# Order of 32 experts written out by hand: first products of one expert around the second products of the one before

## Chip, cores, metric

One core of a Trainium2 chip runs the whole program. Times are device microseconds (us) of one execution; lower is better. Engines: TensorE (PE; its weight loads are PEld), VectorE (DVE), ScalarE (ACT), GpSimd (POOL) and SyncE (SP), which issues the transfers of the weights.

## What is computed

The program is a block of mixed attention with a mixture of experts, and two further layers behind it. The change lies in the mixture: 256 tokens, 32 experts, each token goes to 4 of them. Cut to what matters (`expert_block` works on a block of an expert's tokens):

```python
def expert_block(args):
    tok_idx, e = args
    xb = t_pad[tok_idx]
    hb = xb @ w_exp_in[e] + b_exp_in[e]
    g = jnp.minimum(hb[:, :D_FF], SWIGLU_LIMIT)
    u = jnp.clip(hb[:, D_FF:], -SWIGLU_LIMIT, SWIGLU_LIMIT)
    a = g * jax.nn.sigmoid(SWIGLU_ALPHA * g) * (u + 1.0)
    return a @ w_exp_out[e] + b_exp_out[e]
...
y = jnp.einsum('nk,nkd->nd', gate_w, y_slot)
```

Everything is float32; D_MODEL and D_FF are 1024, so `w_exp_in[e]` has 8.4 MB and `w_exp_out[e]` 4.2 MB. All 32 experts are read once: 403 MB of the 593 MB that the program reads.

## The kernel before

**Work of one expert.** An expert takes up to 64 tokens (CAP). `gather` (L873) picks the tokens' columns out of h1 with matmuls by a selection that VectorE makes, for two experts at a time; the result `xg` is the stationary operand of the first products. `expert` (L905) then does, in the order of its code: `spread_sel` (L892: the selection `sd` back to the tokens with the gate weights, on VectorE, two transposes, a copy `sTs`); the bias into two PSUM banks `pg` and `pu` (L767, 8 matmul instructions); the first products (L915), 64 instructions over four weight tiles `tin`; the clamped SwiGLU (L932 to L938: gc, sg, sg, uc, uc, four on VectorE and one on ScalarE); four transposes of uc (L943, `aT`) and their copy `aTs` (ScalarE, L946); the second products (L951, `py`), 32 instructions over two weight tiles `tout`; their copy `ys` (L954); and the combination (L959, `pc`), 8 instructions whose four banks VectorE adds to `facc` (L964; facc lies in the tensor bcs). A float32 matmul is two instructions in the trace, and the two halves of 64 columns run beside each other.

**Buffers.** PSUM has four banks with tag "b" and four with tag "g" (`pg` and `pu` of two experts). A weight tile is [128, 4096] float32, 2 MB. Eight buffers hold them: `ring` (3), `ring2` (4) and `ring3` (1). `w_exp` (L834) hands out the tiles of an expert, the four tin and then the two tout, and `pick` (L838) takes the buffers by a pattern with period eight; from tile 119 on, ahead of the loop, another pattern. One tile of expert 1 (`spare`, L855) goes into other memory. SP issues the transfers in order (`wload`, L127, L135), and an issue waits until the products that read the buffer's last tile are done.

**What sets the order.** The engines' instructions are put in order by a scheduler at build time; `keep` pins an instruction behind the one traced before it on its engine, and `tc.issue_after(i)` puts a block's instructions behind `i` on its engine. The expert stage pins nearly nothing beside the first eight tiles. `pairs_of` (L1095) calls `expert` for e0 to e1 and puts the gathering for the next pair behind the first quarter of the first products of the pair's first expert. Beside the experts stand: `facc_init` and the gathering for expert 1 (behind the products of expert 0), `later_consts` (L1020, constants on VectorE for later stages, after pair 0), `load_bo` (expert 2), `ln2_rows` (expert 4, rows spread by matmuls, L994) and `out_bias` (expert 6, L1006).

**The loop.** An expert with more than 64 tokens needs further blocks. A loop `tc.For_i(0, n_over, 1)` (L1126) stands after expert 19; its number of iterations is read from the chip, and is 0 for these inputs. Its weight tiles go into `ring2`, all four buffers of it, so ahead of it only three tiles of expert 20 are asked for (L1123), all in `ring`:

```python
    xg = pairs_of(0, 20, xg)
    got = [f() for f in w_exp(20)[0:3]]
    ...
    with tc.For_i(0, n_over, 1) as it:
        ...
        tin, tout = w_all(w_exp(eo, only2=True))
        ...
    pairs_of(20, NE, xg, got)
```

Behind expert 31 the sums of its combination start from facc by matmuls (`take_sum`, L923), and three tiles of the next stage follow (L1146).

Of the kernel before, what the change touches and what calls it, by code (L numbers as in the profile page):

```python
# [9 lines left out]
F32 = mybir.dt.float32  # L10
# [8 lines left out]
NE = 32  # L19
# [53 lines left out]
def tile_kernel(  # L73
# [691 lines left out]
    def expert_bias(p, oh, q, pin=lambda i: i, halves=(0, 1)):  # L765
        for hv in halves:
            pin(T.matmul(p[64 * hv:64 * hv + 64, :], oh[:, q + hv:q + hv + 1].to_broadcast([128, 64]), bi,  # L767
                         start=True, stop=False))

    def first_bias(e, i, halves=(0, 1)):  # L770
        expert_bias(first_acc[e][i], ident[:, 4 * e:4 * e + 4], 2 * i, keep, halves)
# [62 lines left out]
    def w_exp(e, only2=False):  # L834
        wi = w_exp_in[0, e] if isinstance(e, int) else w_exp_in[0, ds(e, 1)].rearrange("o k n -> (o k) n")
        wo_ = w_exp_out[0, e] if isinstance(e, int) else w_exp_out[0, ds(e, 1)].rearrange("o k n -> (o k) n")

        def pick():  # L838
            if only2:
                return ring2  # L840
            m = n_tile[0]
            n_tile[0] += 1
            return (ring2, ring, ring2, ring2, ring, ring3, ring, ring2)[m % 8] if m < 119 else (
                ring, ring, ring, ring2, ring2, ring3, ring2, ring2)[(m + 1) % 8]

        def tin(i):
            return wload(wi[i * 256:(i + 1) * 256, :].rearrange("(p r) n -> p r n", r=2), "p (r n) -> p r n", r=2,
                         pool=pick(), pin=not only2 and n_tile[0] <= 8,
                         parts=2 if isinstance(e, int) and e == NE - 1 and i > 1 else 1)

        def tout(i):
            return wload(wo_[i * 512:(i + 1) * 512, :].rearrange("(p r) n -> p r n", r=4), "p (r n) -> p r n", r=4,
                         pool=pick(), pin=not only2 and n_tile[0] <= 8,
                         parts=4 if isinstance(e, int) and e == NE - 1 and i == 1 else 1)

        def spare():
            src = wi[512:768, :].rearrange("(p r) n -> p r n", r=2)
            a = x_tm.rearrange("p t n -> p (t n)")
            b = [wsp.tile([128, 1024], F32, tag="wl", name="ws") for _ in range(2)]
            keep(nc.sync.dma_start(a, src[:, 0]))  # L860
            for q in range(2):
                keep(nc.sync.dma_start(b[q], src[:, 1, 1024 * q:1024 * (q + 1)]))
            return Spare(a, b)

        if isinstance(e, int) and e == 1:
            return [lambda: tin(0), lambda: tin(1), spare, lambda: tin(3)] + [lambda i=i: tout(i) for i in range(2)]
        return [lambda i=i: tin(i) for i in range(4)] + [lambda i=i: tout(i) for i in range(2)]

    def w_all(ld):
        w = [f() for f in ld]  # L870
        return w[0:4], w[4:6]

    def gather(rank_aps, pin=lambda i: i):  # L873
# [8 lines left out]
        for hf in range(2):  # L882
# [7 lines left out]
        return xg  # L890

    def spread_sel(rank_ap, gate_ap):  # L892
        sd = tmp("sd", 256).rearrange("p (t s) -> p t s", t=2)
# [4 lines left out]
        p2_ = bank("sT")  # L898
        for t in range(2):
            T.transpose(p2_[:, t * 128:(t + 1) * 128], sd[:, t], ident)  # L900
        sT = tmp("sTs", 256)
        S.copy(sT, p2_[:, 0:256])
        return sT

    def expert(xg, a, sel_, oh, tin, tout, mid=None, acc=None, sums=None, ahead=None):  # L905
        sT = sel_()
        pg_, pu_ = acc or (bank("pg", "g"), bank("pu", "g"))
        if acc is None:
            expert_bias(pg_, oh, 0)
            expert_bias(pu_, oh, 2)  # L910
        for i in range(4):
            for r, p, b0 in ((0, pg_, 0), (0, pu_, 1024), (1, pg_, 0), (1, pu_, 1024)) if i < 3 else (
                    (0, pg_, 0), (1, pg_, 0), (0, pu_, 1024), (1, pu_, 1024)):
                for hv in range(2):
                    up = T.matmul(p[64 * hv:64 * hv + 64, :], xg[:, 2 * i + r, a * 64:(a + 1) * 64],  # L915
                                  tin[i][:, r, b0 + hv * 512:b0 + (hv + 1) * 512], start=False, stop=i == 3 and r == 1)
            if i == 0:
                mark["up"] = up.ins
        last = up.ins
        mark["ups"] = last  # L920
        if mid:
            mid()
        def take_sum(t, after):  # L923
            if sums is not None:
                with tc.issue_after(after):
                    for j in range(2):
                        p = bank("pc", "bg"[t])
                        T.matmul(p, ident, facc[:, t, j * 512:(j + 1) * 512], start=True, stop=False)
                        sums[t, j] = p
        take_sum(0, last)  # L930
# [5 lines left out]
        uc = tmp("uc")  # L936
        V.tensor_scalar(uc, pu_, -7.0, 7.0, op0=ALU.max, op1=ALU.min)
        V.scalar_tensor_tensor(uc, uc, 1.0, sg, op0=ALU.add, op1=ALU.mult)  # L938
        if ahead:
            ahead()  # L940
        p = bank("aT")
        for r in range(4):
            last = T.transpose(p[:, r * 128:(r + 1) * 128], uc[:, r:512:4], ident)  # L943
        take_sum(1, last.ins)
        aT = tmp("aTs")
        S.copy(aT, p)  # L946
        py = bank("py")
        for i in range(2):
            for r in range(4):
                for j in range(2):  # L950
                    T.matmul(py[64 * j:64 * j + 64, :], aT[:, r * 128 + i * 64:r * 128 + (i + 1) * 64],  # L951
                             tout[i][:, r, j * 512:(j + 1) * 512], start=i == 0 and r == 0, stop=i == 1 and r == 3)
        ys = tmp("ys")
        S.copy(ys, py)  # L954
        for t in range(2):
            pc = []
            for j in range(2):
                p = sums[t, j] if sums else bank("pc")
                T.matmul(p, sT[64 * j:64 * j + 64, t * 128:(t + 1) * 128], ys[64 * j:64 * j + 64, :],  # L959
                         start=not sums, stop=True)  # L960
                pc.append(p)
# [4 lines left out]
    xg = gather([rr[:, :, 0]], keep)  # L966
# [111 lines left out]
    sums, xg1 = {}, []  # L1078

    def after_first():  # L1080
        with tc.issue_after(mark["up"]):
            xg1.append(gather([rr[:, :, 1]]))
        facc_init()

    last_acc, last_sel = [], []

    def before_last():
        ee = NE - 1
        with tc.issue_after(mark["ups"]):
            last_acc.extend([bank("pg", "g"), bank("pu", "g")])  # L1090
            for i in range(2):
                expert_bias(last_acc[i], ident[:, 4 * ee:4 * ee + 4], 2 * i)
            last_sel.append(spread_sel(rr[:, :, ee], gw[:, :, ee]))

    def pairs_of(e0, e1, xg, got=None):  # L1095
        for e in range(e0, e1, 2):
            nxt = None
            for a in range(2):
                ee = e + a
                ld = w_exp(ee)  # L1100
                if got is not None:
                    w = got + [f() for f in ld[3:]]
                    got = None
                    tin, tout = w[0:4], w[4:6]
                else:
                    tin, tout = w_all(ld)
                if ee == 1:
                    xg = xg1.pop()
                mid = {0: after_first, 2: load_bo, 4: ln2_rows, 6: out_bias}.get(ee)
                acc = first_acc[ee] if ee < 2 else last_acc if ee == NE - 1 else None  # L1110
                expert(xg, a if e else 0, last_sel.pop if ee == NE - 1 else lambda: spread_sel(rr[:, :, ee], gw[:, :, ee]),
                       ident[:, 4 * ee:4 * ee + 4], tin, tout, mid, acc, sums if ee == NE - 1 else None,
                       before_last if ee == NE - 2 else None)
                if a == 0 and e + 2 < NE:
                    with tc.issue_after(mark["up"]):
# [530 lines left out]
```

## Time and profile before

| | |
|---|---|
| median of 3 runs | 1942.14 us (1937.34 to 1943.22) |
| profiled execution | 1934.46 us |
| its span, first to last instruction | 1932.7 us |
| TensorE busy | 1845.3 us, 95% |
| VectorE, ScalarE, GpSimd busy | 814.0, 556.6, 91.7 us |
| mean granted TensorE clock | 0.985 of full speed |
| read from memory | 593.24 MB, 307 GB/s over the span |

Times inside the profile count from the span's start. "PE pc L959" is the instruction of line 959 that writes pc. A busy share of the matmuls is not their peak: they are pipelined, and neighbours overlap in the records. "x4" behind a row counts merged instructions; a merged row's time runs from the first start to the last end. The expert stage lasts from about 250 to 1222 us.

### The profile page before, as it was taken

How to read it: one execution, taken by the hardware profiler on the slowest of the kernel's cores; microseconds unless marked ns; L12 is line 12 of the kernel's file. 1: busy time of each engine (PE TensorE's matmuls, PEld its weight loads, DVE VectorE, ACT ScalarE, POOL GpSimd, SP SyncE). 2: the span in 40 equal slices, each digit the busy share in tenths (PEclk: the TensorE clock that was granted, in tenths of full speed). 3: DMA queues.
4: the chain of work that ended last, by engine and by line, in shares of the span. 5: the costliest groups of instructions: out<-in, count | busy, mean ns of one | idle time of the engine just before them, and what ended most of it. 6: DMA issues, size and time to landing. Idle time of an engine off the chain costs nothing.

```text
span 1932.7 us, 23544 instructions
## 1 busy us (share of the span) xinstructions
PE 1845.3 (95%) x9861; PEld 1130.0 (58%) x9861; DVE 814.0 (42%) x1452; ACT 556.6 (29%) x869; POOL 91.7 (5%) x106
## 2 busy tenths in 40 slices
PE   7999999999999999979999999899999998999999
PEld 6867743343334434324334433589888876678997
DVE  6755733122221222212122121667655565676555
ACT  4645310110010000000000000454544454564443
POOL 3000100000000000000000000100100011001000
PEclk9989999999999999989999999999999999999999
DMA  8667879999999999959999999674576566434452
GB/s 289 242 218 271 345 295 405 404 365 366 430 423 424 425 427 428 426 208 430 428 427 427 428 428 419 251 262 175 198 258 253 218 226 212 160 115 170 174 194 90
DMA packets 100303, 595.86 MB, mean 308 GB/s; under 512 B 7533, under 2 KB 8002, under 8 KB 75362
## 3 DMA queue, kind: packets, MB, share of 16 engines
q1 hardware_dynamic: 85874, 540.68, 69.6%
q0 software_dynamic: 14288, 53.63, 7.9%
q8 instruction: 79, 1.29, 0.3%
q14 instruction: 30, 0.25, 0.0%
q10 hardware_dynamic: 32, 0.01, 0.0%
HBM read 593.24 MB, written 1.06 MB: 307 GB/s over the span
## 4 chain that ended last, share of the span: by engine, by line
PE 79%; DVE 7%; issue 6%; DMA 5%; ACT 3%; POOL 1%; SPq 0%; DVEq 0%; POOLq 0%; ACTq 0%
PE pg L915 12%; PE py L951 12%; PE pu L915 9%; PE xg L887 3%; DMA wa<-in_ada_w_dram 3%; PE hid L271 3%; PE hid L270 3%; PE hid L269 3%; PE pc L959 3%; PE acc L254 3%; PE acc L255 3%; PE acc L256 3%; PE pu L767 2%; PE adp L628 2%; PE aT L943 1%
## 5 line engine op out<-in xcount | busy, mean ns | idle before, releaser
L199 DVE TENSOR_TENSOR wl<-w,wh 128x1024 fp32r<-128x1024 f32 x244 | 301.3, 1236 | 230.8 <-ACT wh L198 230.3
L198 ACT CAST wh<-w 128x1024 fp32r<-128x1024 f32 x244 | 255.9, 1049 | 315.8 <-PE acc L256 85.2
L915 PE MATMUL pg<-w,xg 128*64 128x512 f32 x1016 | 289.2, 602 | 0.0
L915 PE MATMUL pu<-w,xg 128*64 128x512 f32 x1016 | 286.4, 597 | 0.0
L951 PE MATMUL py<-w,aTs 128*64 128x512 f32 x1024 | 231.0, 598 | 3.0 <-ACT aTs L946 3.0
L964 DVE TENSOR_TENSOR bcs<-bcs,pc 128x512 f32<-128x512 f32 x124 | 77.0, 682 | 299.1 <-PE pc L959 299.1
L932 DVE TENSOR_SCALAR gc<-pg 128x512 f32<-128x512 f32 x32 | 22.1, 692 | 406.3 <-PE pg L915 406.3
L951 PEld LDWEIGHTS py<-w,aTs 128*64 128x64 f32 x1024 | 99.0, 137 | 123.9 <-issue 104.4
L915 PEld LDWEIGHTS pu<-w,xg 128*64 128x64 f32 x1016 | 82.6, 138 | 146.7 <-issue 146.6
L915 PEld LDWEIGHTS pg<-w,xg 128*64 128x64 f32 x1016 | 79.9, 138 | 137.3 <-issue 136.9
L270 PE MATMUL hid<-xhl,wh 128*128 128x256 f32 x512 | 145.2, 284 | 0.0
L271 PE MATMUL hid<-xhl,wl 128*128 128x256 f32 x512 | 145.1, 283 | 0.0
L269 PE MATMUL hid<-xhl,wh 128*128 128x256 f32 x512 | 145.0, 284 | 0.0
L934 ACT ACTIVATE sg<-gc 128x512 f32<-128x512 f32 x32 | 20.2, 630 | 389.1 <-DVE gc L932 389.1
L269 PEld LDWEIGHTS hid<-xhl,wh 128*128 128x128 f32 x512 | 98.2, 192 | 2.1 <-ACT xhl L1213 1.7
L270 PEld LDWEIGHTS hid<-xhl,wh 128*128 128x128 f32 x512 | 98.3, 192 | 1.4 <-issue 0.8
L271 PEld LDWEIGHTS hid<-xhl,wl 128*128 128x128 f32 x512 | 98.3, 192 | 0.8 <-issue 0.8
L254 PE MATMUL acc<-wh,hh 128*128 128x512 f32 x240 | 94.5, 395 | 0.0
L255 PE MATMUL acc<-wl,hh 128*128 128x512 f32 x240 | 93.7, 390 | 0.0
L256 PE MATMUL acc<-wh,hh 128*128 128x512 f32 x240 | 93.7, 390 | 0.0
L954 ACT COPY ys<-py 128x512 f32<-128x512 f32 x32 | 18.7, 585 | 236.9 <-PE py L951 236.9
L959 PE MATMUL pc<-ys,sTs 64*128 64x512 f32 x256 | 63.6, 615 | 19.5 <-ACT ys L954 19.5
(529 smaller groups left out, 2761.7 us busy)
## 6 DMA issues: line engine op xcount, KB each, us to landing
w<-in_w_exp_in_dram SPq DMA_DIRECT2D x125, 2048.0 KB, 13.1
w<-in_w_exp_out_dram SPq DMA_DIRECT2D x63, 2048.0 KB, 12.1
w<-in_mlp_w_dram SPq DMA_DIRECT2D x32, 2048.0 KB, 7.7
wa<-in_ada_w_dram POOLq DMA_DIRECT2D x38, 1024.0 KB, 7.4
w<-in_w_in_dram SPq DMA_DIRECT2D x9, 2048.0 KB, 10.5
w<-in_w_in_ab_dram SPq DMA_DIRECT2D x7, 2048.0 KB, 23.3
w<-in_w_qkv_dram SPq DMA_DIRECT2D x6, 2048.0 KB, 7.9
wa<-in_ada_w_dram POOLq DMA_DIRECT2D x20, 512.0 KB, 4.8
```

What stands on the lines that cost most here:

```text
L198: mark["S"] = S.copy(hi, src).ins
L199: mark["V"] = V.tensor_tensor(lo, src, hi.bitcast(F32), op=ALU.subtract).ins
L254: T.matmul(outs[t], hs, wh[:, j, :], start=a, stop=False)
L255: T.matmul(outs[t], hs, wl[:, j, :], start=False, stop=False)
L256: T.matmul(outs[t], ls, wh[:, j, :], start=False, stop=z)
L269: T.matmul(o, hs, xh[:, k + j, :], start=a, stop=False, skip_group_check=True)
L270: T.matmul(o, hs, xl[:, k + j, :], start=False, stop=False, skip_group_check=True)
L271: last = T.matmul(o, ls, xh[:, k + j, :], start=False, stop=z and m % 2 == 1, skip_group_check=True)
L915: up = T.matmul(p[64 * hv:64 * hv + 64, :], xg[:, 2 * i + r, a * 64:(a + 1) * 64], tin[i][:, r, b0 + hv * 512:b0 + (hv + 1) * 512], start= ...
L951: T.matmul(py[64 * j:64 * j + 64, :], aT[:, r * 128 + i * 64:r * 128 + (i + 1) * 64], tout[i][:, r, j * 512:(j + 1) * 512], start=i == 0 a ...
L959: T.matmul(p, sT[64 * j:64 * j + 64, t * 128:(t + 1) * 128], ys[64 * j:64 * j + 64, :], start=not sums, stop=True)
L964: V.tensor_tensor(f, f, pc[j], op=ALU.add)
```

## The change

`pairs_of` and `expert` go; their parts become functions of their own (`up_tile`, `swiglu`, `down_turn`, `down_tile`, `evict`, `combine`, and the two halves of `gather`), and `step(e)` calls them in this order, all matmuls pinned: bias of e; first quarter of the first products of e; on odd e the first half of the gathering for e + 1 and e + 2; transposes of uc of e - 1; second quarter of e; transposes of the selection of e - 1; both second-product tiles of e - 1; third quarter of e; second half of the gathering; combination of e - 1; fourth quarter of e; SwiGLU of e and its selection. Step 32 has only what belongs to expert 31. The weight tiles are asked for in that order (in 0, in 1, out 0 and out 1 of the expert before, in 2, in 3), all pinned on SP, with one pattern of buffers over the whole stage. The loop moves behind step 20 and uses `ring3` alone; ahead of it the six tiles of step 21 and the first of step 22 are asked for. uc and sd of expert 20 go into buffers of another pool over the loop. `spread_sel` makes its selection with two VectorE operations instead of four. The diff, cut:

```diff
+    def pick():
+        m = n_tile[0]
+        n_tile[0] += 1
+        return (ring2, ring, ring3, ring2, ring, ring2, ring, ring2)[m % 8]
...
+    def step_tiles(e):
+
+        out = [("in", e, 0), ("in", e, 1)] if e < NE else []
+        out += [("out", e - 1, i) for i in range(2)] if e else []
+        return out + ([("in", e, 2), ("in", e, 3)] if e < NE else [])
...
         for t in range(2):
-            for d_ in range(2):
-                V.tensor_scalar(sd[:, t, d_ * 64:(d_ + 1) * 64], slot_i, rank_ap[:, t:t + 1], gate_ap[:, t:t + 1],
-                                op0=ALU.is_equal, op1=ALU.mult)
...
+            V.tensor_scalar(sd[:, t].rearrange("p (d s) -> p d s", d=2), slot_i[:, None, :].to_broadcast([128, 2, 64]),
+                            rank_ap[:, t:t + 1], gate_ap[:, t:t + 1], op0=ALU.is_equal, op1=ALU.mult)
...
+    def step(e):
+
+        w = {key: get(key) for key in step_tiles(e)}
+        d = downs.pop(e - 1, None)
+        nxt = None
+        if e < NE:
+            acc = first_acc[e] if e < 2 else (bank("pg", "g"), bank("pu", "g"))
+            if e > 1:
+                eb = bias_sel(ident[:, 4 * e:4 * e + 4])
+                expert_bias(acc[0], eb, 0, keep)
+                expert_bias(acc[1], eb, 1, keep)
+            xg, a = xgs.pop(e)
+            up_tile(acc, xg, a, 0, w["in", e, 0], keep)
+            if e == 0:
+                with tc.issue_after(mark["up"]):
+                    xg_, nxt = gather([rr[:, :, 1]], keep)
+                xgs[1] = xg_, 0
+            elif e % 2 and e + 1 < NE:
+                with tc.issue_after(mark["up"]):
+                    xg_, nxt = gather([rr[:, :, e + 1 + b] for b in range(2)], keep)
+                xgs[e + 1], xgs[e + 2] = (xg_, 0), (xg_, 1)
+        if nxt:
+            nxt(0)
+        if d:
+            uc, turn = d
+            aT = down_turn(uc, keep)
+        if e < NE:
+            up_tile(acc, xg, a, 1, w["in", e, 1], keep)
+        else:
+            take_sum(1)
+        if d:
+            sT = turn()
+            py = bank("py")
             for i in range(2):
...
+                down_tile(py, aT, i, w["out", e - 1, i], keep)
+            ys = evict(py)
+        if e < NE:
+            up_tile(acc, xg, a, 2, w["in", e, 2], keep)
+        if nxt:
+            nxt(1)
+        if d:
+            combine(sT, ys, sums if e == NE else None, keep)
+        if e < NE:
+            up_tile(acc, xg, a, 3, w["in", e, 3], keep)
+            if e == NE - 1:
+                take_sum(0)
+            held = aside if e == 20 else tmp
+            downs[e] = swiglu(acc, held), spread_sel(rr[:, :, e], gw[:, :, e], keep, held)
+
+    for e in range(21):
+        step(e)
+        if e == 0:
+            facc_init()
+            later_consts()
+        elif e in (2, 4, 6):
+            {2: load_bo, 4: ln2_rows, 6: out_bias}[e]()
+    for key in step_tiles(21) + step_tiles(22)[0:1]:
+        get(key)
     with tc.issue_after(mark["SP"]):
         n_over = nc.values_load(ti[0:1, 16:17], min_val=0, max_val=15)
     with tc.For_i(0, n_over, 1) as it:
...
+        for i in range(4):
+            up_tile(acc, xo, 0, i, tin(eo, i, ring3, False))
...
+    for e in range(21, NE + 1):
+        step(e)
     w_ahead = [wcols(w_in_ab_2[0], 2048, 512), wcols(w_in_ab_2[0], 1536, 512), wcols(w_in_ab_2[0], 2560, 512)]
```

## Rows read from the trace of the kernel before

**Rows 1.** The page, part 1: busy time and share of the span.
```profile
PE 1845.3 (95%) x9861; PEld 1130.0 (58%) x9861; DVE 814.0 (42%) x1452; ACT 556.6 (29%) x869; POOL 91.7 (5%) x106
```
**Rows 2.** Busy us by stretches; last three columns: granted clock, DMA share, GB/s.
```profile
253.00:330.00 77.00, 75.78 (x372) 31.83 (x370) 25.27 (x72) 7.38 (x14) 1.04 (x3) 1.00 0.95 380
380.00:480.00 100.00, 96.94 (x424) 40.42 (x420) 22.71 (x49) 10.42 (x19) 0.00 (x0) 0.95 0.92 370
600.00:800.00 200.00, 193.44 (x902) 80.46 (x900) 44.31 (x96) 18.43 (x34) 0.00 (x0) 1.00 1.01 426
820.00:865.00 45.00, 33.32 (x162) 13.39 (x158) 8.62 (x16) 3.83 (x7) 0.00 (x0) 0.93 0.53 194
866.00:1190.00 324.00, 312.14 (x1453) 126.08 (x1454) 67.24 (x148) 28.95 (x54) 0.00 (x0) 0.99 1.01 428
```
**Rows 3.** Chain of waits over one pair of experts: start, length, what.
```profile
561.23 1.01 PE pg L915 x4
...
610.40 6.88 PE py L951 x32
...
620.35 1.01 PE pg L915 x4
```
**Rows 4.** Timeline of the pair's second expert, from its bias on.
```profile
606.41 1.03 PE L767 MATMUL pg<-bi,ident 128*64 128x512 f32 x4
...
607.63 0.69 DVE L938 SCALAR_TENSOR_TENSOR uc<-uc,sg 128x512 f32<-128x512 f32 x1
...
607.65 1.07 PE L767 MATMUL pu<-bi,ident 128*64 128x512 f32 x2 [0.21 <-DVE uc L937]
...
608.65 0.75 PE L943 MATMUL aT<-ident,uc 128*128 128x128 f32 x4
...
609.33 1.07 PE L767 MATMUL pu<-bi,ident 128*64 128x512 f32 x2
...
610.08 7.19 PE L951 MATMUL py<-w,aTs 128*64 128x512 f32 x32
...
618.00 1.99 PE L959 MATMUL pc<-ys,sTs 64*128 64x512 f32 x8 [0.73 <-ACT ys L954]
```
**Rows 5.** Transfers issued from 560 to 700: KB each, median us to landing.
```profile
w<-in_w_exp_in_dram SPq DMA_DIRECT2D x18, 2048.0 KB, 11.5
```
**Rows 6.** Waits of SP's queue, 600 to 800: us in total, times, longest.
```profile
SPq L135 <- PE pu L915: 112.6, 27, 10.1
```
**Rows 7.** Timeline of SP: first issue after expert 0 has started.
```profile
253.45 0.33 SPq L135 DMA_DIRECT2D w<-in_w_exp_in_dram  x1
```
**Rows 8.** Chain of waits, 226 to 480: constants, row broadcasts, bias of the output.
```profile
310.17 0.60 DVE ib L1036
...
317.82 0.57 PE pg L915
...
381.73 3.33 PE row L994 x6
...
445.45 2.77 PE fi L1006 x6
```
**Rows 9.** Timeline around the loop, 853 to 868.
```profile
853.09 10.14 SPq L135 DMA_DIRECT2D w<-in_w_exp_in_dram  x2
...
863.50 1.97 PE L767 MATMUL pg<-bi,ident 128*64 128x512 f32 x2 [7.73 <-DVE sd L896]
...
867.79 0.95 PE L915 MATMUL pg<-w,xg 128*64 128x512 f32 x1
```
**Rows 10.** Waits of SP's queue, whole span: at the loop.
```profile
SPq L1126 <- DMA w<-in_w_exp_in_dram: 6.4, 1, 6.4
```
**Rows 11.** Busy us from 860 to 870, columns as in rows 2.
```profile
860.00:870.00 10.00, 6.50 (x18) 1.91 (x20) 0.98 (x4) 0.37 (x1) 0.00 (x0) 0.58 0.62 233
```
**Rows 12.** Timeline of the tail of expert 31.
```profile
1209.79 0.74 PE L943 MATMUL aT<-ident,uc 128*128 128x128 f32 x4 [0.21 <-DVE uc L938]
...
1220.01 1.99 PE L959 MATMUL pc<-ys,sTs 64*128 64x512 f32 x8 [0.74 <-ACT ys L954]
```

More of the change, by code (lines that the diff above doesn't have):

```diff
@@ L832, in tile_kernel @@
     n_tile = [0]
[L834 to L867, printed above, removed]
@@ new lines, in tout, with spare @@
+    def tout(e, i, pool=None, pin=True):
+        return wload(rows_out(e)[i * 512:(i + 1) * 512, :].rearrange("(p r) n -> p r n", r=4), "p (r n) -> p r n", r=4,
+                     pool=pool or pick(), pin=pin, parts=4 if isinstance(e, int) and e == NE - 1 and i == 1 else 1)
+    def spare():
+        src = w_exp_in[0, 1][512:768, :].rearrange("(p r) n -> p r n", r=2)
+        a = x_tm.rearrange("p t n -> p (t n)")
+        b = [wsp.tile([128, 1024], F32, tag="wl", name="ws") for _ in range(2)]
+        keep(nc.sync.dma_start(a, src[:, 0]))
+        for q in range(2):
+            keep(nc.sync.dma_start(b[q], src[:, 1, 1024 * q:1024 * (q + 1)]))
+        return Spare(a, b)
@@ L873, in gather, with get @@
+    def step_tiles(e):
+        out = [("in", e, 0), ("in", e, 1)] if e < NE else []
+        out += [("out", e - 1, i) for i in range(2)] if e else []
+        return out + ([("in", e, 2), ("in", e, 3)] if e < NE else [])
+    loaded = {}
+    def get(key):
+        if key not in loaded:
+            kind, e, i = key
+            loaded[key] = spare() if key == ("in", 1, 2) else (tin if kind == "in" else tout)(e, i)
+        return loaded[key]
     def gather(rank_aps, pin=lambda i: i):
@@ L881, in gather, with half @@
         w = 64 * n
-        for hf in range(2):
+        def half(hf):
             p = bank("xg")
@@ L905, in expert @@
[L905 to L930, printed above, removed]
@@ new lines, in up_tile @@
+    def up_tile(acc, xg, a, i, w, pin=lambda i: i):
+        pg_, pu_ = acc
+        for r, p, b0 in ((0, pg_, 0), (0, pu_, 1024), (1, pg_, 0), (1, pu_, 1024)) if i < 3 else (
+                (0, pg_, 0), (1, pg_, 0), (0, pu_, 1024), (1, pu_, 1024)):
+            for hv in range(2):
+                last = pin(T.matmul(p[64 * hv:64 * hv + 64, :], xg[:, 2 * i + r, a * 64:(a + 1) * 64],
+                                    w[:, r, b0 + hv * 512:b0 + (hv + 1) * 512], start=False, stop=i == 3 and r == 1))
+        mark["up"] = last.ins
@@ L964, in expert @@
                 V.tensor_tensor(f, f, pc[j], op=ALU.add)
-    xg = gather([rr[:, :, 0]], keep)
+    xg0, half0 = gather([rr[:, :, 0]], keep)
+    for hf in range(2):
+        half0(hf)
     first_sel = mark["sel"]
@@ L1095, in pairs_of @@
[L1095 to L1115, printed above, removed]
-                        nxt = gather([rr[:, :, e + 2 + b] for b in range(2)])
-            xg = nxt
-            if e == 0:
-                later_consts()
-        return xg
@@ L1122, in tile_kernel, with take_sum @@
[L1122 to L1123 removed]
+    sums, xgs, downs = {}, {0: (xg0, 0)}, {}
+    def take_sum(t):
+        for j in range(2):
+            p = bank("pc", "bg"[t])
+            keep(T.matmul(p, ident, facc[:, t, j * 512:(j + 1) * 512], start=True, stop=False))
+            sums[t, j] = p
+    def step(e):
[30 more added lines that the diff above has]
+            py = bank("py")
+            for i in range(2):
+                down_tile(py, aT, i, w["out", e - 1, i], keep)
[12 more added lines that the diff above has]
+            downs[e] = swiglu(acc, held), spread_sel(rr[:, :, e], gw[:, :, e], keep, held)
```

105 lines of the change are left out of this document (58 added, 47 removed).

## Prediction

> **What bounds the kernel now.** I read the page first: TensorE is busy for 95% of the span [rows 1], which would make it the bound everywhere. Then the busy time by stretches [rows 2]: in the expert stage (253 to 1222 us) the DMA engines are as full as TensorE. From 600 to 800 and from 866 to 1190 they have a share of 1.01 and move 426 and 428 GB/s. In three stretches they don't: 380 GB/s at the start, 370 from 380 to 480, and 194 around the loop (820 to 865). So two resources stand almost level, and the reader has to see which of them ends last. The chain of waits decides it for the steady part: a pair of experts takes 620.35 - 561.23 = 59.12 us, 29.56 an expert, and no link of that chain is a transfer [rows 3]. The timeline shows what is in those 29.56 us [rows 4]. With 0.215 us a matmul instruction (32 in 6.88 us [rows 3]), the four bias matmuls that start at 606.41 end at 607.27, and TensorE waits to 607.65 (0.38); the next two end at 608.08, wait to 608.65 (0.57); two more end at 609.76, wait to 610.08 for aTs (0.32); the second products end at 616.96, wait to 618.00 for ys (1.04). That is 2.31 us of standing per expert, so 27.25 of work.
>
> The DMA side of an expert is six tiles of 2048 KB [rows 5], 2.097 MB each. At 428 GB/s a tile takes 4.90 us, an expert 29.4. Such a tile lands 11.5 us after its issue [rows 5], so one or two others are ahead of it in the queue, while SP waits for buffers that TensorE has yet to free [rows 6]: a transfer has work behind it and TensorE never waits for one. So TensorE sets the pace with 29.56 us, and the transfers would allow 29.4, hardly less. **Hiding all 2.31 us can't bring 74 us over 32 experts;** the steady part alone would give 0.16 us an expert. What can be won are the stretches in which the transfers don't run.
>
> **The change part by part.** I follow two clocks, that of the transfers up to the loop, and that of TensorE behind it.
>
> *Transfers up to the loop.* Eight tiles and the spare one are on the chip when expert 0 starts; the ninth is issued at 253.45, when the first buffer is free [rows 7]. The new order of tiles is the order of use with a period of eight over the eight buffers, so this start stays. A lone transfer needs 1.8 us beside its 4.90: the last tile ahead of the loop is issued at 853.09 [rows 9], SP waits 6.4 us for it after the 0.33 of the issue [rows 10], so it lands at 859.8, 6.7 after its issue. Ahead of the loop the new kernel asks for seven further tiles; counted in its order the last is number 129 (from 0), so 122 are behind the eight. 253.45 + 1.8 + 122 x 4.90 = 853. To it come gaps where TensorE is late in freeing buffers: the constants on VectorE that hold up expert 1 to 2 (310.17 to 317.82, some 6 us beside the additions), the row broadcasts (3.33) and the bias of the output (2.77) [rows 8]. They are not removed. Bounds: 0, since TensorE now gains about 1.8 us a step, and what the kernel before lost there, (428 - 380) / 428 x 77 + (428 - 370) / 428 x 100 = 22 us [rows 2]. I take 8, since the first of the three comes before there is a lead and the others after 4 and 6 steps of it. So tile 129 lands at 861.
>
> The Trainium skill, DMA: Bandwidth & Descriptors (Specifications), gives a fabric ceiling of 435 GB/s; by it a tile would be 4.82 us, an estimate, and the landing 10 us sooner, but two long stretches of the trace agree on 426 to 428.
>
> *TensorE up to there.* Step by step, bias, first products, second products, combination are the same instructions as before, so 27.25 us of work. Each wait gets a cover: uc is needed after the next bias and a quarter of first products, 8 + 16 instructions or 5.2 us, and now ends 1.9 us after the first products (608.32 against 606.41 [rows 4]); aTs and ys each get another quarter (3.4 us) for about 0.3 and 1.0. The selection's four VectorE operations become two, off the path. Unknown is what twice as many switches between kinds of matmul cost. Bounds: 0.25 us below (switches that now stand beside waits), 1.15 above (eight new switches at 0.15, by 1.01 for the first four of a kind against 4 x 0.215 [rows 3]). I take 27.6, near the low end, since the timeline has next to nothing between bias and products when no wait is there. From 250 (253.45 less a quarter of first products, 16 x 0.215), with 21 steps, about 10 less for the first (no second products) and 18 for the work of [rows 8], step 20 ends at 838, before tile 129 has landed. So TensorE stands some 25 us at the loop and loses nothing by it, as the transfers go on meanwhile.
>
> *The loop.* Now three tiles wait for buffers one after the other and the transfers fall to 194 GB/s: 24 us of transfer time lost (45 x (1 - 194 / 428)). After: seven buffers are filled, one is kept for the loop. What is left is the drain: the loop has no iteration here, yet SP and all engines wait for the last landing, and the bias starts at 863.50 [rows 9], 3.7 after it. That stays: 864.7. The first instructions then run at half the clock: 1.97 for two [rows 9], granted clock 0.58 in that stretch [rows 11]; bias and two transposes take 4.3 us instead of 2.0, so 2.3 extra. After a longer stand I bound this at 2.3 to 6 and take 2.3, the only row there is. 867.0.
>
> *TensorE behind the loop.* Seven tiles are there, and TensorE, at 27.6 against 29.4, doesn't run out of them before the end: 61 tiles after the loop land by 861 + 8 + 61 x 4.90 = 1168. Eleven steps: 303.6, to 1170.6. *Tail:* from the end of the last first products to the transposes 2.24 (606.41 to 608.65 [rows 4]), then as before from 1209.79 to 1222.00, 12.2 [rows 12]. That work has no next expert to hide it. End: 1185.0.
>
> SP's three tiles of the next stage now wait for later buffers, behind the last expert's; two land before the end, the third about 4 us after, under 12 us of layer norm: nothing. The bias rows and constants keep their queues (POOL, VectorE), and cost what they did.
>
> **Sum:** 1222.0 - 1185.0 = 37 us. The profiled execution took 1934.5 (1.8 around its span), so 1897.5; the median shown, 1942.1, is 7.7 above it (0.4%), so I give 1942.1 - 37 = 1905. With the bounds: gaps 0 and step 27.0 give 15 less, 1890; gaps 22, step 28.4 and 6 us cold give 27 more, 1932.
>
> **The rivals.**
> 1. *The transfers set the pace to the end.* TensorE is at its low bound and there are no gaps: tile 129 at 853, last landing 1160, 4.5 of tail, so 57 us less: 1885. For it: shares of 1.01; against: TensorE has to be ahead after both [rows 8] stops. 0.10.
> 2. *The order hides little.* The engines other than TensorE keep an order that the scheduler sets, and a step takes 28.4 to 29.5. Then TensorE reaches the loop last (258 + 21 steps), and both sides of the loop are its own: at 29.4 a step it ends at 1222, no gain. 1930 to 1945. Against it: each cover above is two to ten times the wait. 0.12.
> 3. *Head of the line, slower.* With every matmul pinned, one late operand stops all that follows, also products whose tiles are there. Where: the transposes of uc behind the first quarter. VectorE has the four additions of the combination (2.5 us) ahead of the clamp; if the scheduler's order puts them, the selections and the sd behind each other ahead of uc, the 3.3 us of cover are used up. It decides from 29.4 - 27.25 = 2.15 us of waits per step; with 3.5 us, 32 x 1.35 = 43 us slower: 1985. Against it: the additions fit beside the last quarter. 0.08.
> 4. *Clock.* If TensorE waits for tiles in small pieces in the steps ahead of the loop, it might fall to 1.2 GHz, where its 27.25 us would be 54.5; three such steps cost 3 x 25 = 75 us of which the stand at the loop takes 25: some 1955. The rows speak against it: with 2.3 us of waits per expert the granted clock is 1.00 [rows 2], and it fell after 7.7 us without work [rows 9, 11]. The Trainium skill, TensorE: Matmul & The Clock Gate (HAM oscillation), tells of a kernel whose matmuls wait for a transfer between tiles and start cold each time; here the waits would be some 0.3 us. 0.04.
>
> **How the numbers follow.** The forecast has 0.66. About 0.3% (6 us) is what a measurement can tell from no change. Faster: 0.66 + 0.10 + 0.08 of rival 2 = 0.84; same: its other 0.04; slower: 0.08 + 0.04 = 0.12. The range, 1885 to 1932, takes in the forecast's bounds, rival 1 and half of rival 2: 0.82.
>
> **What would show it.** Right: from 820 to 860 about 428 GB/s instead of 194; TensorE idle for 20 to 30 us ahead of the loop, with the transfers running; no wait of TensorE for uc, aTs or ys in the chain; 27 to 28 us a step behind the loop; the last combination near 1185. Wrong: waits on VectorE or ScalarE inside the steps, a granted clock below 0.9 away from the loop, or transfers that stand while buffers are free.

## The result and the profile after

The changed kernel takes **1918.3 us** (median of 5 runs, 1915.92 to 1921.77), the kernel before 1942.14 beside it; ratio **0.9891 [0.9869, 0.9913]**. That is 24 us less where 37 were predicted: faster by more than 0.3%, within the range (1885 to 1932), and 13 us short of the predicted time. The profiled execution took 1921.77 us, the slowest of the five; its span is 1920.0. Against the profiled execution of before, 1934.46, it gains 12.7, and that is the difference which the rows below have to explain.

The page, part 1, of the kernel after. It says as little as [rows 1] did: TensorE is busy for 95% again.

```profile
PE 1833.3 (95%) x9861; PEld 1106.0 (58%) x9861; DVE 799.4 (42%) x1388; ACT 557.3 (29%) x869; POOL 91.1 (5%) x106
```

Busy time by stretches, kernel after, columns as in [rows 2]; the last three lines are shorter stretches on which the reading below rests.

```profile
253.00:330.00 77.00, 71.00 (x341) 30.49 (x343) 18.34 (x57) 7.93 (x15) 1.01 (x3) 0.93 0.79 310
380.00:480.00 100.00, 96.12 (x412) 35.31 (x410) 21.10 (x43) 10.46 (x19) 1.45 (x3) 0.93 0.94 392
600.00:800.00 200.00, 200.00 (x966) 76.31 (x966) 45.53 (x90) 19.74 (x36) 0.00 (x0) 1.00 1.01 428
820.00:865.00 45.00, 34.50 (x164) 12.53 (x160) 11.15 (x20) 3.39 (x6) 0.00 (x0) 0.92 1.01 427
866.00:1190.00 324.00, 303.43 (x1448) 115.21 (x1450) 61.10 (x124) 28.77 (x53) 0.00 (x0) 0.96 0.98 413
...
240.00:260.00 20.00, 19.17 (x72) 11.12 (x69) 9.55 (x52) 1.39 (x5) 1.74 (x2) 0.57 0.20 77
280.00:300.00 20.00, 15.69 (x72) 7.79 (x74) 5.02 (x25) 1.59 (x4) 0.00 (x0) 0.83 0.66 262
460.00:480.00 20.00, 20.00 (x76) 7.52 (x77) 2.06 (x3) 1.48 (x3) 0.00 (x0) 0.78 0.70 266
```

The transfers now run through the stretch of the loop, 427 GB/s instead of 194, as predicted. But from 253 to 330 they move 310 GB/s, less than the 380 of before. The last three lines show where they stand, and each has a low granted clock.

The steps, in the chain of waits of the kernel after (start, length, what), where [rows 3] were for before:

```profile
505.81 7.02 PE py L953 x32
...
561.23 7.02 PE py L953 x32
```

These are the second products of one expert and of the second one behind it. Two steps take 561.23 - 505.81 = 55.42, so 27.71 each (before 29.56, predicted 27.6). Waits of TensorE by cause, from 250 to 1207 (us in total, times, longest); beside two short ones of the row broadcasts (1.0 and 0.6) this is all that is left.

```profile
PE pg L771 <- issue: 30.9, 1, 30.9
PE xg L895 <- DVE sel L886: 5.9, 1, 5.9
PE fi L1015 <- DVE gTs L1011: 2.2, 1, 2.2
PE pg L922 <- DMA w<-in_w_exp_in_dram: 1.2, 1, 1.2
PE pc L966 <- ACT ys L958: 1.0, 1, 1.0
```

The waits for uc and aTs of [rows 4] are gone, and of those for ys one is left, that of the last expert. The two stops and the start, in the timeline of the kernel after; the first line answers to [rows 7].

```profile
259.13 9.37 SPq L135 DMA_DIRECT2D w<-in_w_exp_in_dram  x3
...
284.23 4.09 PE L895 MATMUL xg<-sel,h 128*128 128x128 f32 x16 [5.93 <-DVE sel L886]
...
457.45 5.94 PE L1015 MATMUL fi<-bo,gTs 32*128 32x512 f32 x8 [2.22 <-DVE gTs L1011]
...
463.32 1.98 PE L771 MATMUL pg<-bi,ident 128*64 128x512 f32 x4
```

The first buffer is free 5.7 us later than before. At 278 TensorE stands 5.9 us for the selections of the next pair: VectorE has the constants of `later_consts` ahead of them. At 455 it stands 2.2 for a copy; then the eight instructions of the output's bias take 5.94, and behind them four take 1.98, half speed, until 469. In the kernel before the same job is split around a quarter of first products (439.85 to 448.2); the new order has it whole between two steps.

The loop in the chain of waits, and then the end of the stage in the timeline, kernel after ([rows 9, 12] before):

```profile
850.20 35.36 DMA w<-in_w_exp_in_dram
885.56 1.01 issue
886.57 1.98 PE pg L771 x4
```

```profile
894.67 2.15 PE L895 MATMUL xg<-sel,h 128*128 128x128 f32 x16
...
1190.54 1.89 PE L922 MATMUL pu<-w,xg 128*64 128x512 f32 x8
...
1205.13 1.99 PE L966 MATMUL pc<-ys,sTs 64*128 64x512 f32 x8 [1.02 <-ACT ys L958]
```

The last transfer ahead of the loop lands at 885.56 and TensorE goes on at 886.57, 21.9 later than predicted (864.7). The stage ends at 1207.12 instead of the predicted 1185.0, 22.1 later; behind it lie 712.9 us, 2.2 more than before (710.7). These 24.3 are what lacks of the 37 in this pair of executions. The profiled execution of before was 7.7 us faster than its median and that of after 3.5 slower, so between the medians 13 lack.

### The profile page after: what moved, and what is told of

It reads as the page before. It is cut to its first block, busy times and chain, and to the rows that moved or that the text cites. A ratio compares the mean times of both kernels' runs of the same rounds, so it can differ in the third digit from the quotient of the medians.

```text
span 1920.0 us, 23489 instructions
## 1 busy us (share of the span) xinstructions
PE 1833.3 (95%) x9861; PEld 1106.0 (58%) x9861; DVE 799.4 (42%) x1388; ACT 557.3 (29%) x869; POOL 91.1 (5%) x106
## 4 chain that ended last, share of the span: by engine, by line
PE 80%; DMA 8%; issue 5%; DVE 4%; POOL 1%; ACT 1%; SPq 0%; POOLq 0%; DVEq 0%; ACTq 0%
PE pg L922 11%; PE py L953 11%; PE pu L922 11%; PE xg L895 4%; DMA w<-in_w_exp_in_dram 4%; DMA wa<-in_ada_w_dram 3%; PE hid L271 3%; PE hid L270 3%; PE hid L269 3%; PE pc L966 3%; PE acc L254 3%; PE acc L255 3%; PE acc L256 3%; PE adp L628 2%; PE pu L771 2%
## 5 line engine op out<-in xcount | busy, mean ns | idle before, releaser
L922 PE MATMUL pg<-w,xg 128*64 128x512 f32 x1016 | 262.0, 605 | 1.2 <-DMA w<-in_w_exp_in_dram 1.2
L922 PE MATMUL pu<-w,xg 128*64 128x512 f32 x1016 | 257.1, 595 | 0.0
L953 PE MATMUL py<-w,aTs 128*64 128x512 f32 x1024 | 226.8, 595 | 0.0
L922 PEld LDWEIGHTS pu<-w,xg 128*64 128x64 f32 x1016 | 73.6, 138 | 147.1 <-issue 147.1
L922 PEld LDWEIGHTS pg<-w,xg 128*64 128x64 f32 x1016 | 67.8, 138 | 139.0 <-issue 131.6
L953 PEld LDWEIGHTS py<-w,aTs 128*64 128x64 f32 x1024 | 70.7, 137 | 133.2 <-issue 132.7
L897 ACT COPY xg<-xg 128x512 f32<-128x512 f32 (+1 forms) x34 | 19.0, 560 | 265.8 <-PE xg L895 265.8
L895 PEld LDWEIGHTS xg<-sel,h 128*128 128x128 f32 x544 | 71.3, 208 | 33.9 <-issue 33.5
L895 PE MATMUL xg<-sel,h 128*128 128x128 f32 (+1 forms) x544 | 77.7, 300 | 6.0 <-DVE sel L886 5.9
```

Of the source, the lines that this page charges most:

```text
L922: last = pin(T.matmul(p[64 * hv:64 * hv + 64, :], xg[:, 2 * i + r, a * 64:(a + 1) * 64], w[:, r, b0 + hv * 512:b0 + (hv + 1) * 512], start ...
L953: pin(T.matmul(py[64 * j:64 * j + 64, :], aT[:, r * 128 + i * 64:r * 128 + (i + 1) * 64], w[:, r, j * 512:(j + 1) * 512], start=i == 0 and ...
```

## Experiments

All times are medians, ratios are to the kernel before on the same chip. A time "against the changed kernel" is against 1918.3. The column on the right is the start of the last combination of the stage in the profiled run, 1220.01 before and 1205.13 after. Behind it, where no run changes anything, the profiled executions take another 711.9 to 720.6 us, so a few us between two times say little of the stage.

| run | us | ratio | last combination |
|---|---|---|---|
| e1_loop_only | 1935.41 | 0.9974 [0.9955, 0.9993] | 1215.34 |
| e2_three_tiles | 1911.8 | 0.9841 [0.981, 0.9871] | 1199.84 |
| e3_no_loop | 1909.17 | 0.9839 [0.9807, 0.987] | 1192.69 |
| e4_side_late | 1902.26 | 0.9806 [0.9774, 0.9838] | 1182.70 |
| e5_late_three | 1892.69 | 0.9742 [0.9715, 0.9768] | 1174.22 |
| e6_consts_alone | 1911.17 | 0.9839 [0.9815, 0.9864] | 1197.35 |
| e7_bias_alone | 1914.1 | 0.985 [0.9822, 0.9879] | 1196.02 |
| e8_old_tiles | 1933.7 | 0.995 [0.9936, 0.9964] | 1212.00 |
| e9_late_noloop | 1892.75 | 0.9749 [0.9724, 0.9774] | 1175.88 |
| e10_unpinned | 1959.93 | 1.0085 [1.0054, 1.0116] | 1237.56 |
| e11_before_late | 1945.81 | 1.0018 [0.9998, 1.0037] | 1221.29 |

### The loop alone, on the kernel before

```diff
             if only2:
-                return ring2
+                return ring3
...
-            return (ring2, ring, ring2, ring2, ring, ring3, ring, ring2)[m % 8] if m < 119 else (
-                ring, ring, ring, ring2, ring2, ring3, ring2, ring2)[(m + 1) % 8]
+            return (ring2, ring, ring2, ring2, ring, ring2, ring3, ring)[m % 8]
...
-    got = [f() for f in w_exp(20)[0:3]]
+    got = [f() for f in w_exp(20)] + [w_exp(21)[0]()]
```

> The kernel before with one part of the change: the loop uses the one-buffer pool, and ahead of it seven tiles are asked for (six of expert 20, one of 21); the order of the products stays. Theory (TensorE sets the pace at 29.56 us an expert, the transfers hardly less; the lost 24 us of transfer time at the loop were slack): 0 to 6 us faster than before, some 1937, and TensorE still idle for 2.3 us per expert. Rival (the transfers set the pace, so the loop's lost transfers are the whole gain): 18 to 24 us faster, about 1920.

Windows and waits of this run:

```profile
820.00:865.00 45.00, 33.45 (x158) 13.69 (x160) 8.62 (x16) 4.11 (x8) 0.00 (x0) 0.90 0.92 382
```

```profile
PE pg L767 <- DVE sd L895: 7.8, 1, 7.8
```

The transfers run on, 382 instead of 194 GB/s, and TensorE waits 7.8 us at the loop, as before (7.73, [rows 9]). 5 us are gained by the ratio, which fits the theory (0 to 6). As long as TensorE sets the pace with 29.56 us a step, transfers that run through the loop are worth next to nothing.

### The order without its pins, and the order without its tiles

e10_unpinned: in `step`, no matmul is pinned. The program order, the tiles and the order on SP stay.

```diff
-            up_tile(acc, xg, a, 0, w["in", e, 0], keep)
+            up_tile(acc, xg, a, 0, w["in", e, 0])
...
-            aT = down_turn(uc, keep)
+            aT = down_turn(uc)
```

> The changed kernel with the same program order of step(e), but its matmuls not pinned, so that the scheduler sets their order at build time. Theory: it is the program order and the order of the tiles that carry the gain; the scheduler leaves the order nearly as written (most of the differences lie in the first steps), a step stays at 27.6 to 27.8 us and the time within 6 us of 1918. Rival: without pins the waits for uc, aTs and ys come back, 1 to 2 us a step: 1930 to 1945.

Chain of waits and, below it, waits by cause of this run:

```profile
602.77 1.98 PE pc L966 x6
...
664.27 1.98 PE pc L966 x6
```

```profile
PE pc L966 <- ACT ys L958: 16.8, 23, 0.7
...
PE pu L771 <- DVE uc L937: 5.1, 20, 0.5
PE aT L944 <- DVE uc L938: 4.2, 3, 2.0
PE xg L895 <- DVE sel L886: 2.9, 8, 0.4
PE fi L1015 <- DVE gTs L1011: 0.4, 1, 0.4
```

The theory is wrong. Of two steps, which take 664.27 - 602.77 = 61.50, each has 30.75 us, 3 more than with pins and more than the 29.56 of before. The scheduler's order puts the combination right behind the second products and the transposes between the two halves of the bias, so TensorE waits for ys, uc and uc again. These waits are not the whole 3 us: TensorE is busy for 59.19 of the 61.50, against 55.42 of 55.42 in two steps of the changed kernel, so 1.2 us a step are waits and 1.9 lie in longer busy time of as many instructions (269 and 270). Part of that is the combination, which takes 1.98 + 1.12 us in two pieces instead of 1.99 in one; the rest stays open. The rival had the mechanism and too small a price: 1960, slower than before. From the loop to 1017 the order is nearly as written, and the second products in the chain follow each other by 27.7 us; then it slips again.

e8_old_tiles: the order of products as changed and pinned, the tiles fetched in the order of before, each expert's out tiles behind its in tiles.

```diff
-        out = [("in", e, 0), ("in", e, 1)] if e < NE else []
-        out += [("out", e - 1, i) for i in range(2)] if e else []
-        return out + ([("in", e, 2), ("in", e, 3)] if e < NE else [])
+        out = [("in", e, i) for i in range(4)]
+        return out + [("out", e, i) for i in range(2)] if e < NE else []
...
-                down_tile(py, aT, i, w["out", e - 1, i], keep)
+                down_tile(py, aT, i, get(("out", e - 1, i)), keep)
...
-    for key in step_tiles(21) + step_tiles(22)[0:1]:
+    for key in step_tiles(21)[0:3]:
```

> The changed kernel's order of products, with the weight tiles fetched in the order of before (four in tiles and two out tiles of one expert, the out tiles of step e issued one step ahead of their use), and the first three tiles of step 21 ahead of the loop: as many as the changed kernel has then issued. Theory: the order of the tiles matters only as far as a buffer is given back later than its turn; two out tiles sit in buffers for some half step longer, which takes about two tiles (9.8 us) from the 39 us by which eight buffers run ahead, and the transfers still keep up: 1918 within 6 us. Rival: tiles that are issued out of the order of use make TensorE wait in each step, some 1 to 2 us a step over 31 steps: 1945 to 1975.

(The count in the expectation was off by two: this kernel has issued 129 tiles ahead of the loop, the changed one 131.) Waits of TensorE, first from 600 to 870, then from 884 to 1215:

```profile
PE pg L921 <- DMA w<-in_w_exp_in_dram: 11.7, 8, 2.9
...
PE pg L921 <- DMA w<-in_w_exp_in_dram: 6.7, 5, 3.1
```

15 us slower than the changed kernel, between the two theories' numbers: TensorE waits not in each step, but in 13 places, all behind 600. The transfers move 427 GB/s from 600 to 860 and 426 from 900 to 1180, so it isn't bandwidth. The order of the tiles would explain it, though no run shows it by itself: an in tile that is needed now lies behind two out tiles that are needed half a step later, 9.8 us of transfers. Where TensorE goes on behind the loop, in the chain of waits:

```profile
884.14 1.98 PE pg L771 x4
```

That is 2.4 us earlier than in the changed kernel (886.57), with two tiles fewer ahead of the loop; so the 11.7 us of waits ahead of it cost no time by themselves, they come out of the stand at the loop (14.1 instead of 30.9). The last combination starts 6.9 later, so 9.3 us are lost behind the loop, 6.7 of them in the waits above. The other 5.7 of the 12.6 us between the two profiled executions lie behind the stage and stay open. So without its pins the order loses 17 us against before, and without its tiles it keeps 10 of its 24.

### What the loop still costs

e2_three_tiles asks for three tiles ahead of the loop instead of seven; e3_no_loop has no loop (the further blocks of an expert with more than 64 tokens are left out; these inputs have none).

```diff
-    for key in step_tiles(21) + step_tiles(22)[0:1]:
+    for key in step_tiles(21)[0:3]:
```

> The changed kernel, but ahead of the loop three tiles are asked for instead of seven. Theory (the drain at the loop's entry waits for the last landing; with three tiles that comes at 864 instead of 883, just after TensorE has ended step 20 at 858, and behind the loop five buffers are free at once): TensorE stands about 9 us instead of 29, the stage ends at about 1190 instead of 1207, total about 1905, 14 us faster than the changed kernel. Rival (the prediction's: transfers that are not asked for ahead of the loop are lost, up to 4 x 4.9 us): the stage ends 10 to 20 us later, total 1928 to 1938.

> The changed kernel without the loop (it leaves out the further blocks of experts with more than 64 tokens, of which these inputs have none). Theory (at the loop the transfers lose some 8 us, TensorE 29, and behind it TensorE is the later of the two): without it the transfers set the end: last landing near 1175 to 1180, stage end near 1183, total about 1897, 20 us faster than the changed kernel. Rival (the 29 us of standing cost nothing, as the transfers go on through it): 8 us faster, about 1910.

Waits of TensorE, e2_three_tiles and then e3_no_loop:

```profile
PE pg L771 <- DMA w<-in_w_exp_out_dram: 11.0, 1, 11.0
```

```profile
PE pg L922 <- DMA w<-in_w_exp_in_dram: 13.6, 12, 1.8
```

With four tiles less in front of it the loop holds TensorE 11.0 us instead of 30.9, and the time falls by 6.5 against the changed kernel; without the loop by 9. That is less than the theory gave in both (14 and 20); in e3_no_loop the rival's 8 is the nearer. The four tiles have to come behind the loop instead, and in e3_no_loop TensorE waits for tiles in small pieces to the end, 13.6 us in 12 places. So the stand at the loop was on the path, but of its 31 us only some 10 could be won.

### The side work

e4_side_late moves the four side jobs from steps 0, 2, 4, 6 to steps 9, 11, 13, 15; e6 and e7 move one alone; e11 moves them in the kernel before, whose order is otherwise untouched.

```diff
             facc_init()
-            later_consts()
-        elif e in (2, 4, 6):
-            {2: load_bo, 4: ln2_rows, 6: out_bias}[e]()
+        elif e in (9, 11, 13, 15):
+            {9: load_bo, 11: later_consts, 13: ln2_rows, 15: out_bias}[e]()
```

> The changed kernel with the work beside the experts later: the constants on VectorE behind step 11 instead of 0, the row broadcasts behind step 13 instead of 4, the bias of the output behind step 15 instead of 6. Theory (in the first seven steps TensorE has no lead over the transfers, so each stop there takes transfer time that never comes back, 23 us of it between 260 and 480; later a lead of 10 to 20 us covers the same stops): the last landing ahead of the loop at about 863 instead of 883, total about 1898, 20 us faster than the changed kernel. Rival (the stops cost the same wherever they are): within 3 us of the changed kernel, 1918.

Windows of e4_side_late, columns as above, and its chain of waits at the loop:

```profile
240.00:260.00 20.00, 19.52 (x104) 10.41 (x105) 10.34 (x54) 1.86 (x6) 2.84 (x3) 0.89 0.52 188
280.00:300.00 20.00, 20.00 (x100) 8.05 (x98) 5.58 (x10) 1.88 (x4) 0.00 (x0) 1.00 0.90 361
460.00:480.00 20.00, 20.00 (x94) 6.81 (x94) 5.12 (x10) 1.59 (x3) 0.00 (x0) 1.00 1.00 426
600.00:700.00 100.00, 97.19 (x439) 37.57 (x436) 22.38 (x47) 11.35 (x21) 1.96 (x4) 0.96 1.01 427
```

```profile
834.59 29.75 DMA w<-in_w_exp_in_dram
864.34 1.10 issue
865.44 1.98 PE pg L771 x4
```

The same instructions, seven to eleven steps later, and 16 us less against the changed kernel, nearer the theory's 20 than the rival's 3. TensorE still stops (in the last of the four windows it is busy 97.19 of 100, at a granted clock of 0.96), but the transfers don't notice: 427 GB/s. By step 9 TensorE has run some 9 x (29.4 - 27.7) = 15 us ahead of the transfers, and a stop eats from that (an estimate from the two step times). The loop is left at 865.44, 21.1 earlier, of which 5.2 are the start (188 instead of 77 GB/s in the first window: 20 x 111 / 428).

> The changed kernel with the loop's constants alone moved from behind step 0 to behind step 11. Theory: their place ahead of the selections on VectorE costs the stop at 279 us with the half clock behind it (4.7 + 2.1 us of transfers in the windows 280:300 and 300:320, against e4_side_late) and the late start (5.2 + 0.7 us in 240:260 and 260:280): the loop is left about 12.7 us earlier, near 874, and the time is about 1905.5. Rival: the late start is chance and not the constants: 1911.

> The changed kernel with the output biases alone moved from behind step 6 to behind step 15. Theory: the stop at 457 us and the half clock behind it cost 7.6 us of transfers (266 instead of 428 GB/s in the window 460:480), which come back: loop left about 879, about 1910.7 us. Rival: a stop there is only moved, and the transfers lose the same at step 15: 1918.

Loop left at 879.47 with the constants moved alone and at 878.76 with the bias moved alone, 7.1 and 7.8 earlier than in the changed kernel; in time 7.1 and 4.2 less. The first time fits its rival: the late start is not the constants' doing (the profiled run of e6_consts_alone has it too, 100 GB/s from 240 to 260). And the stop at the output's bias costs nearly as much without the one at the constants, as a window of e6_consts_alone shows; 20 x (428 - 299) / 428 = 6.0 us of transfers, against 7.6 in the changed kernel:

```profile
460.00:480.00 20.00, 20.00 (x100) 7.91 (x98) 0.00 (x0) 2.07 (x4) 0.00 (x0) 0.97 0.78 299
```

The time of e7_bias_alone lies half way between its theory's and its rival's, while its loop was left where the theory put it. The intervals of the two overlap, so which job costs how much stays open.

> The kernel before, with its side work moved as in e4_side_late (constants behind pair 10, bias rows at expert 9, row broadcasts at 13, output bias at 15). Theory: TensorE's own stops set the pace of the kernel before, so a stop costs it the same wherever it stands: within 6 us of before. Rival: the stops early in the stage cost the transfers their lead in the kernel before as well, and moving them gives some 12 to 18 us: 1925 to 1931.

No gain in the kernel before: 1.0018 [0.9998, 1.0037]. Its transfers stop at the new places instead, as its windows show:

```profile
600.00:700.00 100.00, 94.56 (x419) 37.09 (x415) 26.83 (x75) 10.53 (x19) 1.98 (x4) 1.00 0.97 404
700.00:800.00 100.00, 97.21 (x446) 41.10 (x446) 24.01 (x49) 9.05 (x17) 0.00 (x0) 0.98 0.96 395
```

In the kernel before, a step of TensorE (29.56) is longer than its transfers (29.4), so it never has a lead to spend, and a stop costs the same wherever it stands. What makes a late stop free is the change itself.

### Both together

> The side work at steps 9 to 15 as in e4_side_late, and three tiles instead of five fetched ahead of the loop. Theory: what the loop costs is the time TensorE stands while the tiles issued ahead of it land (25.4 us in e4_side_late); two tiles less are 9.8 us less, so the loop is left at about 855.6 instead of 865.44, and the stage ends 5 to 10 us earlier than the 1183.9 of e4_side_late, since the transfers then set the end (864.3 + 1.8 + 63 x 4.9 = 1174.8 for the last tile): 1892 to 1898 us. Rival: the transfers set the end of e4_side_late already, and nothing is left: 1902.

> The side work at steps 9 to 15 and no loop at all (the further blocks of an expert with more than 64 tokens are left out; there are none in these inputs). Theory: behind the start the transfers then set the pace to the end, and what is left of the loop's price in e5_late_three is the time in which they move 311 instead of 427 GB/s in the window 840:860, 5.4 us: 1886 to 1889. Rival: TensorE sets the end in e5_late_three, and the loop costs nothing there any more: 1892.7 within 2 us.

e5_late_three has the edits of e4_side_late and e2_three_tiles. (The expectation counted five tiles ahead of the loop where there are seven; four less are 19.6 us, and the loop was left 20.8 earlier.) Chain of waits of e5_late_three at the loop and at the end of the stage:

```profile
818.66 25.43 DMA w<-in_w_exp_out_dram
844.09 0.59 issue
844.68 1.98 PE pg L771 x4
...
1115.54 33.46 DMA w<-in_w_exp_out_dram
...
1174.22 1.18 PE pc L966 x4
```

**1892.69 us, 0.9742 [0.9715, 0.9768]:** the best version here, 50 us below before and within the theory's 1892 to 1898. TensorE waits 5.5 us at the loop. The last transfer in the chain lands at 1149.00, 25 us ahead of the last combination, and from 976 on TensorE waits for tiles in 11 places, 9.7 us in all: the transfers set the pace. Without any loop (e9_late_noloop) the time is the same, 1892.75, as its rival said; its profiled run had the late start (first issue 259.19, against 252.91 in e5_late_three), so whether an undisturbed pair would differ by the theory's 5 us isn't settled.

## Why the prediction was right and where it was wrong

**Right: what bounds it, and what the order does.** That hiding all waits alone wins little because the transfers stand level, and that the loop's stretch is where time comes from: 427 instead of 194 GB/s. (e1_loop_only shows that the loop alone wins little; the new order with the loop as it was has not been run.) The step: 27.71 measured against 27.6 taken. TensorE goes on at 886.57; with 2.9 us for the cold clock added, as the prediction counts, the eleven steps take 1192.43 - 889.5 = 302.9 against 303.6. The cold clock: bias and a quarter of first products, 24 instructions, took 8.10 (886.57 to 894.67) instead of 24 x 0.215 = 5.16, so 2.9 against 2.3. The tail: 14.7 against 14.4. Rival 2 (the order hides little) did not come; in e10_unpinned, where TensorE's own order slips, its waits are back. Rival 3 did not come where it was looked for, since no wait for uc is left. But its mechanism, one late operand that stops all that is pinned behind it, is what the two stops are, at the selections and at the output's bias: without pins the same waits are 0.4 us at most (the last two lines of e10_unpinned's waits, against 5.9 and 2.2). Rival 1 (the transfers set the pace to the end) is what e5_late_three became; rival 4's low clock came, but behind the stops and not in the steps.

**Wrong: the step "transfers up to the loop", by its term "gaps", 8 with bounds 0 and 22.** Two things. The first issue was put at 253.45, "so this start stays"; it came at 259.13, 5.7 later. The start comes early or late from run to run, so this part is bad luck unless the new order favours the late one, which is open (last section). And the gaps: resuming 3.7 after the landing, as the prediction counts, gives 886.57 - 3.7 - 259.13 - 1.8 - 122 x 4.90 = 24.1 instead of 8, just above the upper bound. (The 3.7 did not stay either: the chain has the landing at 885.56, 1.0 ahead, and with it the gaps are 26.8. In the kernel before the first bias behind the loop waited for sd as well [rows 9].)

By the windows: (428 - 262) / 428 x 20 = 7.8 at the constants and 7.6 at the bias of the output, the half clock behind them included; the rest lies in the stretches beside them (344 GB/s from 300 to 320, 3.9 us) and in the first 20 us. The prediction had the right places, and said "before there is a lead" of the first, yet took a value near the low end for the others "after 4 and 6 steps". Six steps of 1.7 are 10 us, and the two jobs need more than the 3.33 and 2.77 of [rows 8]. The row broadcasts hold TensorE from 391.87 to 397.86, 6.0 us. The bias of the output costs 2.2 of standing, 5.9 of work and some 2.8 by the half clock up to 469, together 11 by this estimate, where 4 of lead are left; the missing 7 fit the 7.6. That the stop at the constants had spent the lead is not the cause, as e6_consts_alone shows. The prediction had also left out that the clock falls there. Of the 22.1 us by which the stage ended too late, these two make 5.7 + 16.1 = 21.8.

e4_side_late is the test of it: without the early stops, and with the early start, the loop is left at 865.44, where 864.7 was predicted, and the time is 1902.26, where 1905 was. That the two agree so well is partly luck. By the same count e4_side_late still has gaps of 865.44 - 3.7 - 253.98 - 1.8 - 122 x 4.90 = 8.2, with none of the three stops early (3.1 of it from 280 to 300, at 361 GB/s; no run says why). So the stops cost 24.1 - 8.2 = 15.9, twice the whole term, and the 8 us that the prediction set aside for them are as many as the run loses to gaps that it did not see.

**Half wrong: the stand at the loop, of which "TensorE [...] loses nothing by it".** The transfers do go on meanwhile, but behind the loop TensorE sets the pace, so the end moves with the landing. e2_three_tiles and e3_no_loop won 6.5 and 9 us there. The prediction compared the last landing (1168) with TensorE's last first products (1170.6) and saw no slack; the last tile is needed only half way through the second products of the last expert, 8 us later (after: 1197.02 + 3.5 against 1192.43). So some 10 us stood to be won at the loop, which is what these two runs found.

## What to carry to other kernels

Where an engine and the transfers are nearly level, a reorder that makes the engine faster pays through the lead that it builds, a little per step: put what stops the engine behind the steps that build it, and count the half clock behind a stop as part of the stop. In a pinned order one late operand stops everything behind it, so look for such operands in the side work too, not only in the steps. An order written by hand needs its pins and the tiles in the same order; either alone gave a fraction or a loss here. A barrier behind prefetched tiles costs the landing of all of them: prefetch only as many as land while the engine still has work.

## What was not expected of the hardware

Around the bias of the output the granted clock falls: 0.69 from 458 to 460, 0.50 from 460 to 468. TensorE had stood for 2.2 us ahead of that (455.23 to 457.45), although 2.31 us of short waits in each step of the kernel before left the clock at 1.00 [rows 2]. But the stand isn't needed. In e10_unpinned the same eight instructions, behind a wait of 0.36 us, are followed by half the clock too:

```profile
456.00:462.00 6.00, 6.00 (x14) 1.48 (x14) 1.18 (x2) 0.00 (x0) 0.00 (x0) 0.50 0.64 270
```

In the kernel before, behind a wait of 0.51 us, it is 0.66 from 448 to 450 and 0.50 from 450 to 452. What about this job lowers the clock is not shown.

And the start differs between runs whose instructions are the same up to there: the gathering of expert 0 took half as long in e4_side_late as in e9_late_noloop. In the chain of waits of e4_side_late, then e9_late_noloop:

```profile
246.40 3.95 PE xg L895 x32
```

```profile
247.53 7.02 PE xg L895 x32
```

The clock was at its full level of 2.4 GHz in one (1.00 from 246 to 250) and at 1.2 in the other (0.50 from 250 to 256), and the first weight buffer came free at 253.98 and at 259.19. In e9_late_noloop it had been at 1.00 from 243 to 246, while TensorE stood 3.1 us for the tile M, and fell again behind that. Of the 13 profiled executions seven start early (first issue at 252.91 to 256.83, a wait for M of 0.5 to 0.8 us) and six late (259.13 to 261.84). Four of the six have a wait for M of 2.8 to 3.1; the changed kernel and e8_old_tiles have 0.8 and 0.9 and start late all the same. All three with the order of before start early, and four of the ten with the new one, so whether the new order favours the late start isn't settled. What decides was not found; it moves the whole transfer-bound stage by 5 us.
